# Adding the sums of squares on VectorE instead of GpSimd in a two-block transformer kernel

## The chip, the core and the metric

The program runs on one core of a Trainium2 chip. The core has engines that run side by side and wait for each other through semaphores: TensorE (PE in the rows; PEld is its weight load), VectorE (DVE), ScalarE (ACT), GpSimd (POOL) and SyncE (SP, which here only issues DMAs). The metric is the device time of one execution in microseconds, as the median of three.

## What is computed

Two transformer blocks in float32 on 256 tokens of width 1024. The first has a mixer with two attentions and a gated feed-forward with a short convolution; the second has a linear recurrence (`hgrn2_mixer`), a SwiGLU, a block attention (`moba_mixer`) and another SwiGLU. What matters here is that each section ends in a residual sum and begins with a norm over the 1024 features, so that a sum of squares over features is wanted at each border:

```python
def rms_norm(x, g):
    xf = x.astype(jnp.float32)
    y = xf * lax.rsqrt(jnp.mean(xf * xf, axis=-1, keepdims=True) + RMS_EPS)
    return (y * g.astype(jnp.float32)).astype(x.dtype)

def second_block(...):
    h = rmsnorm_of_first_block            # the first block ends in a norm of its own
    for layer in range(2):
        y = rms_norm(h, norm_mix[layer])
        y = hgrn2_mixer(y, ...) if layer == 0 else moba_mixer(y, ...)
        h = h + y
        h = h + swiglu(rms_norm(h, norm_ffn[layer]), w13[layer], w2[layer])
    return rms_norm(h, final_norm)
```

Inside `hgrn2_mixer` the output of the recurrence is normed in the same way (`rms_norm(o, out_norm)`).

## The kernel before

The residual `h` stays in SBUF turned over: features on the partitions, tokens along the free axis, as 8 slices of 128 x 256. Matrix products are made of three passes with a high and a low half of each operand (`mm3`, or `proj_w` with the halves of the input side by side). A weight block of 128 x 1024 is fetched by a DMA of SP into a buffer `f`, ScalarE writes its high half and VectorE its low half (`r<-f` on ACT, then `r<-f,r` on DVE, both 128 x 1024). `Weights` asks for these blocks some way ahead.

Six sections follow each other: `mixer1`, `ffn` with the convolution, `mixer2` (the recurrence), `ffn`, `mixer3`, and a last `ffn`, which ends in `finish` and is not touched. The other five end in `end`. It adds four pieces of the result to `h` (DVE, `h<-ps,h`, after a factor in `mixer2`), writes the high half of the next section's input, times the gain, on ACT and its low half on DVE (`r<-h,vec,r`; 128 x 256, eight of them), and calls `squares`: ACT squares `h` in four pieces of 128 x 512, three adds bring them to one, `over_partitions` adds its two halves (128 x 256) and lets TensorE sum over the partitions by 16 small passes with a column of ones (`ps<-ones,f`), `mean_rsqrt` makes the factor of each token with some ten tiny VectorE steps (`fs`, 128 x 2), and `bcast` spreads it over the partitions by two matmuls (`ps<-f,ones`). The next section's matmuls need the halves of the input at once, and the factor only later, on their results.

Before the change these adds are GpSimd's, 3 x 128 x 512 and one 128 x 256 at each of the five ends. At the end of the first `ffn` the norm of the first block and the first norm of the second come together: `squares` is called twice there, and the second call's adds are VectorE's already. In `mixer2`, three more GpSimd adds of 128 x 512 join the squares of the four pairs of heads, and `over_partitions` is VectorE's there.

No order is written by hand: every instruction is first recorded (`Trace.add`), with the earlier ones it depends on, and then `schedule` plays all of them through a list scheduler, where each has a price (`price`) and the older one goes first when two are ready. What comes out is the order of each engine's queue, and each queue runs strictly in that order on the chip. GpSimd's adds have the price

```python
            op.cost = 1000 + 4 * n if len(reads) > 1 else 150 + 2.1 * n
```

in ns for n elements of the free axis, VectorE's `69 + 1.042 * n`. A recorded instruction may be held behind one more: while `nc.floor` is set to an instruction, all that are recorded depend on it. `store_rel`, which builds the table of attention biases for `mixer3` with DMAs of GpSimd and one product on TensorE, is held in this way behind the last GpSimd instruction of `mixer1`.

All instructions are issued in `emit`, and so the profile gives nearly all of them the line L434; they are told apart by their tiles and sizes.

Of the kernel before, what the change touches and what calls it, by code (L numbers as in the profile page):

```python
# [13 lines left out]
ALU = mybir.AluOpType  # L14
# [467 lines left out]
class Builder:  # L482
# [85 lines left out]
        nc.scalar.activation(b, ps, AF.Copy)  # L568
        return b

    def squares(self, scale=None, eng=None):

        nc = self.nc
        tot = None
        for i in range(4):
            ks = slice(2 * i, 2 * i + 2)
            sq = self.t("f2", 2, SEQ)
            if scale is None:
                nc.scalar.activation(sq, self.h[:, ks, :], AF.Square)
            else:  # L580
                for k in (0, 1):
                    nc.scalar.activation(sq[:, k, :], self.h[:, 2 * i + k, :], AF.Square, scale=scale[:, 2 * i + k:2 * i + k + 1])
            if tot is None:
                tot = sq
            else:
                (eng or nc.gpsimd).tensor_tensor(tot, tot, sq, op=ALU.add)
        return self.over_partitions(tot, eng or nc.gpsimd)

    def over_partitions(self, tot, eng):

        ss, v = self.ps(2), self.t("f1", SEQ)
        eng.tensor_tensor(v, tot[:, 0], tot[:, 1], op=ALU.add)
        for t in range(2):
            for q in range(0, P, 32):
                self.nc.tensor.matmul(ss[q:q + 32, t:t + 1], lhsT=v[:, t * P + q:t * P + q + 32], rhs=self.ones[:, :1],
                                      start=True, stop=True)
        return ss
# [36 lines left out]
    def end(self, accs, g, scale=None, norm=None):  # L634


        nc = self.nc
        X, _ = self.parts(KD)
        if norm is not None:
            both = self.t("fs", KD)  # L640
            nc.vector.tensor_tensor(both, g, norm, op=ALU.mult)
            g = both
        for i in range(4):
            ks = slice(2 * i, 2 * i + 2)
            hv = self.h[:, ks, :]
            add = accs[i]
            if scale is not None:
                add = self.t("f2", 2, SEQ)
                nc.vector.tensor_tensor(add, accs[i], scale[:, None, :].to_broadcast([P, 2, SEQ]), op=ALU.mult)
            nc.vector.tensor_tensor(hv, add, hv, op=ALU.add)  # L650
            for k in (2 * i, 2 * i + 1):
                nc.scalar.activation(X[k][:, 0], self.h[:, k, :], AF.Copy, scale=g[:, k:k + 1])
                nc.vector.scalar_tensor_tensor(X[k][:, 1], self.h[:, k, :], g[:, k:k + 1], X[k][:, 0].bitcast(F32),
                                               op0=ALU.mult, op1=ALU.subtract)
        r = self.mean_rsqrt(self.squares())
        if norm is not None:

            ss, v = self.squares(norm, nc.vector), self.t("fs", 2)
            nc.vector.tensor_tensor(v, r, r, op=ALU.mult)
            nc.vector.scalar_tensor_tensor(v, ss, RS / D, v, op0=ALU.mult, op1=ALU.mult)  # L660
            nc.vector.tensor_scalar(v, v, RS * EPS, None, op0=ALU.add)
            r2 = self.rsqrt(v, 2)
            r1 = self.bcast(r)
            nc.vector.tensor_tensor(r2, r2, r, op=ALU.mult)
            out = X, r2, self.bcast(r2)
            for k in range(KD):
                nc.vector.scalar_tensor_tensor(self.h[:, k, :], self.h[:, k, :], norm[:, k:k + 1], r1, op0=ALU.mult, op1=ALU.mult)
            return out
        return X, r, self.bcast(r)
# [425 lines left out]


    def ffn(self, X, w_up, w_down, conv=False, final=False, **end):

        nc = self.nc
# [56 lines left out]
        if not final:  # L1156
            down(NB - 2, NB - 1)
            return self.end(accs, **end)
# [43 lines left out]
    def mixer2(self, X):  # L1202


        nc, a = self.nc, self.a
        V, A_, T, G = nc.vector, nc.scalar, nc.tensor, nc.gpsimd
# [5 lines left out]
        sq = self.t("f2", 2, SEQ)  # L1212
# [24 lines left out]
        def sides(p):  # L1237
            W = Weights(self, self.rows(w_in, 2 * D + p * 256, 2 * D + p * 256 + 256))
            ps = self.ps(2, 256)
            self.proj_x(W, [ps[:, 0], ps[:, 1]], X, KD, 256, one_bank=True)  # L1240
            it = self.t("f2", 2, 256)
            for t in range(2):
                A_.activation(it[:, t, :], ps[:, t, :], AF.Identity, scale=rs[:, t:t + 1])
            og = proj(3 * D + p * 256)
            A_.activation(og, og, AF.Sigmoid)
            return it, og
# [59 lines left out]
        def outs(p, sc, it, og):  # L1306
            po = self.ps(2, SEQ)
            for e in range(2):
                hc = slice(e * P, (e + 1) * P)
                T.matmul(po[:, e, :], lhsT=it[:, 0, hc], rhs=sc[:, e, :SEQ], start=True, stop=False, skip_group_check=True)  # L1310
                T.matmul(po[:, e, P:], lhsT=it[:, 1, hc], rhs=sc[:, e, SEQ:], start=False, stop=True, skip_group_check=True)
            fin = self.t("f2", 2, SEQ)
            for e in range(2):
                hd = 2 * p + e
                V.scalar_tensor_tensor(fin[:, e, :], po[:, e, :], gon[:, hd:hd + 1], og[:, e, :], op0=ALU.mult, op1=ALU.mult)
            gx, g = self.pair()
            self.hl(g[:, :, 0], g[:, :, 1], fin)
            GO.append(gx)
            if p == 0:
                A_.activation(sq, po, AF.Square)  # L1320
            else:
                o2 = self.t("f2", 2, SEQ)
                A_.activation(o2, po, AF.Square)
                G.tensor_tensor(sq, sq, o2, op=ALU.add)

        for p in range(4):
            sc = scores(p, *front(p))
            outs(p, sc, *sides(p))
        ro = self.bcast(self.mean_rsqrt(self.over_partitions(sq, V)))
        accs = self.new_accs()  # L1330
        for u in range(4):
            self.out_t(accs, w_out, u, GO[u], u == 0, u == 3)
# [78 lines left out]
def build(tc, a, out, stop=None):  # L1411
    with ExitStack() as ctx:
        b = Builder(tc.nc, a, out)

        def stopped(name):
            if stop == name:
                ht = b.tokens()
                for t in range(2):
                    b.nc.sync.dma_start(out[t * P:(t + 1) * P, :], ht[t])
                b.nc.emit(tc, ctx)  # L1420
            return stop == name

        X = b.setup()
        X = b.mixer1(X)
        end = b.nc.last("gpsimd")
        b.late_setup()
        b.nc.floor = end
        b.store_rel()
        b.nc.floor = None
        if stopped("h1"):  # L1430
            return
        if stop == "h2":
            b.ffn(X, a["w_up"][0], a["w_down"][0], conv=True, g=b.vec("norm_mix_2", 0))
            stopped("h2")
            return
        X = b.ffn(X, a["w_up"][0], a["w_down"][0], conv=True, g=b.vec("norm_mix_2", 0), norm=b.vec("norm_final_g"))
        if stopped("x2"):
            return
        X = b.mixer2(X)
        if stopped("h3"):  # L1440
            return
        X = b.ffn(X, a["ffn_w13_2"][0], a["ffn_w2_2"][0], g=b.vec("norm_mix_2", 1))
        if stopped("h4"):
            return
        X = b.mixer3(X)
        if stopped("h5"):
            return
        b.ffn(X, a["ffn_w13_2"][1], a["ffn_w2_2"][1], final=True)
        b.nc.emit(tc, ctx)
# [25 lines left out]
```

## Time and profile before

| | us |
|---|---|
| median of 3 runs (lowest, highest) | 1027.95 (1027.83, 1028.59) |
| the profiled execution | 1028.07 |
| its span, from the first to the last instruction | 1026.3 |
| PE busy in it | 999.1 (97%) |
| DVE, ACT, POOL busy | 774.5, 577.7, 42.6 |

The profile tells for each engine when each instruction began and ended, and what ended the idle time before it. TensorE's matmuls overlap in its pipeline, so that a matmul lasts longer in the rows than the distance to the next one. The views used below are the page's first part, the table of waits, tables of busy time by stretches of the span, groups of equal instructions, and the timeline, in which equal neighbours are one row. The five section ends lie at about 191, 382, 529, 719 and 825 us.

### The profile page before, as it was taken

What the parts mean: (1) busy time and instruction counts of PE and PEld (TensorE: products, weight loads), DVE (VectorE), ACT (ScalarE), POOL (GpSimd) and SP (SyncE); (2) the same over time, 40 slices, a digit from 0 to 9 for tenths busy, and PEclk for the clock granted to TensorE, in tenths of its full rate; (3) what the DMA queues carried; (4) which work ended last, traced back from release to release, by engine and by line L of the source; (5) the groups of instructions that cost most, each with busy time, mean ns of one, the idle gap of its engine ahead of it and who ended that gap; (6) DMA issues with size and microseconds to landing.
All of it is one profiled execution on the core that took longest, in us unless ns stands there. A gap on an engine that the chain in (4) does not pass through costs nothing.

```text
span 1026.3 us, 18746 instructions
## 1 busy us (share of the span) xinstructions
PE 999.1 (97%) x7526; PEld 907.1 (88%) x7526; DVE 774.5 (75%) x1434; ACT 577.7 (56%) x960; POOL 42.6 (4%) x41
## 2 busy tenths in 40 slices
PE   7999999999999999999999999999999999999996
PEld 5887899889999998999998999999889988888885
DVE  6998578699888889876878776767846586576774
ACT  7886646556656576444565445455554655545432
POOL 1000000210000002000011000000200020000000
PEclk9999999999999999999999999999999999999999
DMA  9245367377465663644554765657354745556501
GB/s 333 80 145 184 103 190 225 124 242 242 153 207 187 201 199 90 184 146 138 160 178 144 244 192 180 199 171 226 104 161 149 232 148 153 183 176 196 164 1 42
DMA packets 130152, 173.90 MB, mean 169 GB/s; under 512 B 5842, under 2 KB 112730, under 8 KB 129936
## 3 DMA queue, kind: packets, MB, share of 16 engines
q1 hardware_dynamic: 129312, 169.31, 52.5%
q0 software_dynamic: 752, 3.38, 1.0%
q8 instruction: 59, 0.97, 0.4%
q14 instruction: 29, 0.24, 0.1%
HBM read 171.61 MB, written 2.63 MB: 170 GB/s over the span
## 4 chain that ended last, share of the span: by engine, by line
PE 89%; DVE 9%; issue 1%; ACT 1%; DMA 1%; POOL 0%; DVEq 0%; POOLq 0%; ACTq 0%
PE ps L434 89%; DVE r L434 4%; DVE f L434 3%; DVE fs L434 1%; DVE h L434 1%; DMA f<-in_conv_w_dram 1%; ACT f L434 1%; POOL f L434 0%; ACT r L434 0%; DVEq L434 0%; DVE lb L434 0%; POOLq L434 0%; ACTq L434 0%; POOLq L1462 0%
## 5 line engine op out<-in xcount | busy, mean ns | idle before, releaser
L434 PE MATMUL ps<-r,r 128*128 128x256 f32 (+2 forms) x5998 | 926.4, 314 | 8.1 <-DVE r L434 7.5
L434 PEld LDWEIGHTS ps<-r,r 128*128 128x128 f32 x5998 | 834.3, 190 | 81.9 <-DVE r L434 11.1
L434 DVE TENSOR_TENSOR r<-f,r 128x1024 fp32r<-128x1024 f32 (+3 forms) x369 | 414.3, 1150 | 69.6 <-ACT r L434 33.9
L434 ACT ACTIVATE r<-f 128x1024 fp32r<-128x1024 f32 (+3 forms) x373 | 351.1, 980 | 118.9 <-PE ps L434 54.9
L434 ACT ACTIVATE f<-ps 128x256 f32<-128x256 f32 (+5 forms) x226 | 85.5, 424 | 190.5 <-PE ps L434 190.2
L434 DVE TENSOR_TENSOR f<-ps,f 128x256 f32<-128x256 f32 (+1 forms) x178 | 76.0, 460 | 80.5 <-ACT f L434 64.5
L434 DVE TENSOR_TENSOR f<-f,f 128x512 f32<-128x512 f32 (+3 forms) x153 | 100.6, 658 | 12.1 <-ACT f L434 5.5
L434 ACT ACTIVATE f<-f 128x512 f32<-128x512 f32 (+5 forms) x82 | 45.1, 551 | 49.4 <-DVE f L434 48.9
L434 POOL TENSOR_TENSOR f<-f,f 128x512 f32<-128x512 f32 x18 | 26.9, 1494 | 768.5 <-ACT f L434 459.1
L434 DVE SCALAR_TENSOR_TENSOR f<-f,cw,f 128x255 f32<-128x255 f32 (+1 forms) x88 | 38.3, 480 | 10.8 <-ACT f L434 10.7
L434 PE MATMUL ps<-f,f 128*64 128x128 f32 (+4 forms) x320 | 46.3, 330 | 0.1
L434 PEld LDWEIGHTS ps<-f,f 128*64 128x64 f32 (+3 forms) x320 | 35.7, 168 | 6.7 <-issue 2.1
L434 PE MATMUL ps<-pack,f 128*128 128x128 f32 (+2 forms) x165 | 27.5, 293 | 6.5 <-DMA f<-in_conv_w_dram 3.6
L434 ACT ACTIVATE f<-f,fs 128x256 f32<-128x256 f32 (+3 forms) x50 | 24.3, 489 | 16.7 <-DVE fs L434 16.5
L434 ACT ACTIVATE f<-f,vec,cw 128x256 f32<-128x256 f32 x44 | 23.9, 594 | 16.7 <-DVE f L434 16.7
L434 PEld LDWEIGHTS ps<-pack,f 128*128 128x128 f32 (+2 forms) x165 | 20.2, 147 | 11.1 <-DVE f L434 4.8
L434 DVE CUSTOM_DVE_ANT_0 f<-ps,f 128x256 f32<-128x256 f32 (+1 forms) x48 | 17.8, 399 | 14.2 <-PE ps L434 14.1
L434 ACT ACTIVATE f<-ps,fs 128x512 f32<-128x512 f32 (+3 forms) x28 | 15.9, 597 | 19.9 <-PE ps L434 18.8
L434 DVE SCALAR_TENSOR_TENSOR r<-h,vec,r 128x256 fp32r<-128x256 f32 x32 | 23.3, 763 | 2.0 <-ACT r L434 2.0
L434 ACT ACTIVATE r<-h,vec 128x256 fp32r<-128x256 f32 x32 | 14.5, 500 | 15.9 <-DVE h L434 15.9
L434 DVE TENSOR_TENSOR f<-f,fs 128x512 f32<-128x512 f32 (+6 forms) x46 | 16.6, 389 | 7.2 <-PE ps L434 6.7
L434 PEld LDWEIGHTS ps<-f 128*32 128x32 f32 (+2 forms) x880 | 14.0, 114 | 4.3
(85 smaller groups left out, 244.2 us busy)
## 6 DMA issues: line engine op xcount, KB each, us to landing
f<-in_ffn_w_dram SPq DMA_DIRECT2D x132, 512.0 KB, 4.2
f<-in_w_up_dram SPq DMA_DIRECT2D x44, 512.0 KB, 4.7
f<-in_hgrn_w_in_dram SPq DMA_DIRECT2D x32, 512.0 KB, 4.3
f<-in_w_in_dram SPq DMA_DIRECT2D x26, 512.0 KB, 4.9
f<-in_moba_w_in_dram SPq DMA_DIRECT2D x24, 512.0 KB, 4.5
f<-in_w_down_dram SPq DMA_DIRECT2D x22, 512.0 KB, 4.2
f<-in_w_out_dram SPq DMA_DIRECT2D x8, 512.0 KB, 3.9
f<-in_hgrn_w_out_dram SPq DMA_DIRECT2D x8, 512.0 KB, 3.3
```

The costliest lines, as they stand in the source:

```text
L434: getattr(getattr(self.nc, op.eng), op.fn)(*args, **kwargs)
```

## The change

The adds of `squares`, of `over_partitions` and of the recurrence are issued on VectorE. `squares` notes the last VectorE instruction recorded when it is called and holds its three adds behind that one: in the first call that is the low half of the eighth input slice, in the second call (at the first `ffn`'s end) the last step of the first call's factor. `store_rel` is held behind the last TensorE instruction of `mixer1`, which is the second matmul of `bcast`, instead of the last GpSimd one.

```diff
-    def squares(self, scale=None, eng=None):
+    def squares(self, scale=None):
         nc = self.nc
-        tot = None
+        tot, before = None, nc.last("vector")
...
             if tot is None:
                 tot = sq
             else:
-                (eng or nc.gpsimd).tensor_tensor(tot, tot, sq, op=ALU.add)
-        return self.over_partitions(tot, eng or nc.gpsimd)
-
-    def over_partitions(self, tot, eng):
+                nc.floor = before
+                nc.vector.tensor_tensor(tot, tot, sq, op=ALU.add)
+                nc.floor = None
+        return self.over_partitions(tot)
+
+    def over_partitions(self, tot):
         ss, v = self.ps(2), self.t("f1", SEQ)
-        eng.tensor_tensor(v, tot[:, 0], tot[:, 1], op=ALU.add)
+        self.nc.vector.tensor_tensor(v, tot[:, 0], tot[:, 1], op=ALU.add)
...
-            ss, v = self.squares(norm, nc.vector), self.t("fs", 2)
+            ss, v = self.squares(norm), self.t("fs", 2)
...
-                G.tensor_tensor(sq, sq, o2, op=ALU.add)
+                V.tensor_tensor(sq, sq, o2, op=ALU.add)
...
-        ro = self.bcast(self.mean_rsqrt(self.over_partitions(sq, V)))
+        ro = self.bcast(self.mean_rsqrt(self.over_partitions(sq)))
...
-        end = b.nc.last("gpsimd")
+        end = b.nc.last("tensor")
         b.late_setup()
         b.nc.floor = end
         b.store_rel()
```

The scheduler makes a new order of it. VectorE's queue at the end of `mixer1`, before; `r_83` holds the last two of the eight input slices, `r_92` and `r_81` are low halves of weight blocks, `f_107` is the next section's first result:

```order
L434 TENSOR_TENSOR h_170<-ps_154,h_170 128x512
L434 TENSOR_TENSOR r_87<-f_69,r_95 128x1024
L434 SCALAR_TENSOR_TENSOR r_83<-h_170,vec_182,r_83 128x256 x2
L434 TENSOR_TENSOR r_92<-f_65,r_79 128x1024
L434 TENSOR_TENSOR r_81<-f_64,r_80 128x1024
L434 TENSOR_TENSOR f_107<-ps_157,f_116 128x256
L434 TENSOR_TENSOR f_107<-ps_159,f_121 128x256
L434 TENSOR_SCALAR fs_136<-ps_153 128x2
```

The same place after the change, with the adds into `f_110` and the halves added into `f_121`:

```order
L434 TENSOR_TENSOR h_170<-ps_154,h_170 128x512
L434 TENSOR_TENSOR r_87<-f_69,r_95 128x1024
L434 SCALAR_TENSOR_TENSOR r_83<-h_170,vec_182,r_83 128x256 x2
L434 TENSOR_TENSOR f_110<-f_110,f_103 128x512
L434 TENSOR_TENSOR f_110<-f_110,f_105 128x512
L434 TENSOR_TENSOR r_92<-f_65,r_79 128x1024
L434 TENSOR_TENSOR f_110<-f_110,f_109 128x512
L434 TENSOR_TENSOR f_107<-ps_157,f_125 128x256
L434 TENSOR_TENSOR f_121<-f_110 128x256
L434 TENSOR_TENSOR f_107<-ps_159,f_116 128x256
L434 TENSOR_TENSOR r_82<-f_64,r_80 128x1024
L434 TENSOR_SCALAR fs_136<-ps_153 128x2
```

What stood up to the last input slice stands as it did; the four adds came in behind it, two of them ahead of the first weight half.

VectorE's queue at the end of the first `ffn`, before; `r_94` and `r_97` hold input slices five to eight, `f_103` is the second call's sum:

```order
L434 SCALAR_TENSOR_TENSOR r_94<-h_170,fs_132,r_94 128x256 x2
L434 TENSOR_TENSOR r_89<-f_66,r_82 128x1024
L434 SCALAR_TENSOR_TENSOR r_97<-h_170,fs_132,r_97 128x256 x2
L434 TENSOR_TENSOR r_87<-f_58,r_98 128x1024
L434 TENSOR_TENSOR f_103<-f_103,f_104 128x512
L434 TENSOR_TENSOR r_90<-f_68,r_76 128x1024
L434 TENSOR_TENSOR f_103<-f_103,f_107 128x512
L434 TENSOR_SCALAR fs_138<-ps_159 128x2
L434 TENSOR_TENSOR f_103<-f_103,f_102 128x512
```

After the change, where `r_91` and `r_90` hold these slices and `f_111` is the first call's sum:

```order
L434 SCALAR_TENSOR_TENSOR r_91<-h_170,fs_132,r_91 128x256 x2
L434 TENSOR_TENSOR r_82<-f_65,r_92 128x1024
L434 SCALAR_TENSOR_TENSOR r_90<-h_170,fs_132,r_90 128x256 x2
L434 TENSOR_TENSOR r_97<-f_64,r_81 128x1024
L434 TENSOR_TENSOR f_111<-f_111,f_105 128x512
L434 TENSOR_TENSOR r_84<-f_66,r_98 128x1024
L434 TENSOR_TENSOR f_111<-f_111,f_109 128x512
L434 TENSOR_TENSOR f_111<-f_111,f_110 128x512
L434 TENSOR_TENSOR f_123<-f_111 128x256
L434 TENSOR_TENSOR r_76<-f_68,r_89 128x1024
L434 TENSOR_SCALAR fs_138<-ps_157 128x2
```

The first call's adds took the place of the second call's, which moved behind the tiny steps of the first factor.

TensorE's queue at the end of the second block's first `ffn`, before, around the small passes with the ones:

```order
L434 MATMUL ps_155<-r_87,r_80 128x256 x2
L434 MATMUL ps_155<-r_87,r_96 128x256
L434 MATMUL ps_155<-r_87,r_80 128x256
L434 MATMUL ps_154<-ones_178,f_123 32x1 x8
L434 MATMUL ps_155<-r_87,r_80 128x256
```

After the change:

```order
L434 MATMUL ps_154<-r_80,r_82 128x256
L434 MATMUL ps_156<-r_81,r_79 128x256 x2
L434 MATMUL ps_156<-r_81,r_84 128x256
L434 MATMUL ps_156<-r_81,r_79 128x256 x2
L434 MATMUL ps_156<-r_81,r_84 128x256
L434 MATMUL ps_155<-ones_178,f_123 32x1 x8
```

They stand six matmuls behind the start of a new accumulation now, and stood ten behind it before.

## Rows read from the trace of the kernel before

**Rows 1.** The page's first part: busy us, share of the span, instructions.

```profile
PE 999.1 (97%) x7526; PEld 907.1 (88%) x7526; DVE 774.5 (75%) x1434; ACT 577.7 (56%) x960; POOL 42.6 (4%) x41
```

**Rows 2.** Five section ends: stretch, length, busy PE, PEld, DVE, ACT, POOL; clock, DMA.

```profile
190.85:212.30 21.45, 19.97 (x136) 16.69 (x136) 18.83 (x35) 11.95 (x22) 7.22 (x7) 1.00 0.32 104
382.31:405.60 23.29, 20.85 (x199) 20.28 (x198) 22.24 (x55) 14.77 (x27) 5.64 (x4) 1.00 0.34 100
528.86:551.00 22.14, 20.39 (x139) 17.07 (x138) 20.47 (x37) 12.62 (x22) 5.26 (x4) 1.00 0.45 139
718.61:737.00 18.39, 17.07 (x153) 16.54 (x152) 13.71 (x29) 10.12 (x18) 6.01 (x4) 1.00 0.35 103
825.43:844.00 18.57, 17.08 (x122) 14.69 (x121) 17.55 (x31) 10.66 (x20) 5.87 (x4) 1.00 0.44 131
sum 103.84, PE 95.36 PEld 85.27 DVE 92.79 ACT 60.12 POOL 30.01; mean PE 19.07 PEld 17.05 DVE 18.56 ACT 12.02 POOL 6.00
```

**Rows 3.** The same view, sum over the five stretches between those ends.

```profile
sum 704.40, PE 704.40 PEld 645.75 DVE 515.10 ACT 374.81 POOL 5.53; mean PE 140.88 PEld 129.15 DVE 103.02 ACT 74.96 POOL 1.11
```

**Rows 4.** Table of waits: who waited for whom, us in total, times, longest.

```profile
PE ps L434 <- DVE r L434: 7.5, 8, 1.8
```

**Rows 5.** Timeline, end of `mixer1`: start, us, engine, operation, count, [idle before, releaser].

```profile
195.31 3.75 DVE L434 SCALAR_TENSOR_TENSOR r<-h,vec,r 128x256 fp32r<-128x256 f32 x4
...
195.79 2.98 POOL L434 TENSOR_TENSOR f<-f,f 128x512 f32<-128x512 f32 x2 [179.55 <-DVE r L434]
...
201.24 3.76 PE L434 MATMUL ps<-r,r 128*128 128x512 f32 x19 [1.40 <-DVE r L434]
...
201.50 3.99 DVE L434 TENSOR_TENSOR r<-f,r 128x1024 fp32r<-128x1024 f32 x2
```

**Rows 6.** DVE groups by form: count, busy us, mean ns, idle before.

```profile
L434 DVE TENSOR_TENSOR f<-f,f 128x512 f32<-128x512 f32 x137 | 95.1, 694 | 12.0 <-ACT f L434 5.5 <-PE ps L434 4.6
...
L434 DVE SCALAR_TENSOR_TENSOR r<-h,vec,r 128x256 fp32r<-128x256 f32 x32 | 23.3, 763 | 2.0 <-ACT r L434 2.0
...
L434 DVE SCALAR_TENSOR_TENSOR h<-h,vec,f 128x256 f32<-128x256 f32 x8 | 3.7, 477 | 0.0
```

**Rows 7.** Timeline, end of the first `ffn`.

```profile
386.27 4.21 POOL L434 TENSOR_TENSOR f<-f,f 128x512 f32<-128x512 f32 x3 [162.15 <-ACT f L434]
386.36 0.68 DVE L434 TENSOR_TENSOR h<-ps,h 128x512 f32<-128x512 f32 x1
...
391.49 1.34 DVE L434 SCALAR_TENSOR_TENSOR r<-h,fs,r 128x256 fp32r<-128x256 f32 x2
...
392.49 2.41 PE L434 MATMUL ps<-r,r 128*128 128x256 f32 x18 [1.82 <-DVE r L434]
392.75 1.21 DVE L434 TENSOR_TENSOR r<-f,r 128x1024 fp32r<-128x1024 f32 x1
...
397.61 0.30 PE L434 MATMUL ps<-ones,f 128*32 128x1 f32 x16 [0.62 <-DVE f L434]
```

**Rows 8.** Timeline, end of the second `ffn`.

```profile
731.60 0.31 PE L434 MATMUL ps<-ones,f 128*32 128x1 f32 x16 [0.71 <-POOL f L434]
```

**Rows 9.** Timeline of PE alone, a stretch of equal matmuls.

```profile
385.95 4.60 PE L434 MATMUL ps<-r,r 128*128 128x256 f32 x37
```

**Rows 10.** PE groups by form: count, busy us, mean ns, idle before.

```profile
L434 PE MATMUL ps<-r,r 128*128 128x256 f32 x4340 | 567.1, 284 | 2.4 <-DVE r L434 2.4
L434 PE MATMUL ps<-r,r 128*128 128x512 f32 x1586 | 396.7, 393 | 4.5 <-DVE r L434 4.5
```

**Rows 11.** Busy time of DVE alone, nine tiny steps; stretch, length, busy.

```profile
207.28:209.04 1.76, 1.45 (x11) 1.00 0.82 256
```

**Rows 12.** DMA issues by line: count, KB each, median us to landing.

```profile
f<-in_c_rel_dram POOLq DMA_DIRECT2D x1, 96.0 KB, 4.3
```

**Rows 13.** Timeline of PE alone in `mixer2`, two levels of the recurrence.

```profile
417.88 0.45 PE L434 MATMUL ps<-f 128*32 128x16 f32 x32
...
419.52 0.45 PE L434 MATMUL ps<-f 128*32 128x16 f32 x32
```

## The prediction

> **What bounds the kernel now.** I read the page's first part, then busy time by stretches, then the waits and the timeline. PE is busy for 97% of the span, DVE for 75%, POOL for 4% [rows 1]: the time is PE's, and a change of additions can move it only where PE stands still. The five section ends last 103.84 us and hold 95.36 of PE's work, so 8.48 us of idle time; the stretches between them are 704.40 us long and PE is busy for all of it [rows 2, 3]. Two things follow. What is saved at an end goes straight to the end of the program, for nothing else is late behind it. And a new wait is not absorbed either. PE's granted clock is 1.00 at all five ends, the 2.4 GHz level, so that the stops have not cost clock and none is to be won back.
>
> Nearly all of the 8.48 is nine stops. PE waits 7.5 us for DVE's `r` in eight stops, seven of them here [rows 4]: 1.40 at the end of `mixer1` and 1.82 at the first `ffn`'s are the ones shown [rows 5, 7]. What they wait for is the low half of an input slice. Then there are .62 for the first call's half add, VectorE's work being late [rows 7], and .71 for GpSimd's half add [rows 8]. 7.5 + .62 + .71 is 8.83; one of the eight, about .5, is elsewhere, and 8.3 remain.
>
> Why is the input late? The four `r<-h,vec,r` at the end of `mixer1` took 3.75 us from 195.31 on, while two adds of POOL ran from 195.79 for 2.98 [rows 5]. Their mean over the kernel is 763 ns, while the same operation of the same size with three inputs into `h` takes 477 [rows 6]. Two weight halves, `r<-f,r`, took 3.99 there, and one without POOL beside it 1.21 [rows 5, 7]. Each of these has two inputs in SBUF. `h<-ps,h`, with one input in PSUM, took .68 in the middle of POOL's adds [rows 7]. So DVE's instructions with two SBUF inputs wait for POOL's add to end, and the chain to the input slices, which PE has nothing to do without, is stretched by them.
>
> The Trainium skill says the same in "SBUF — State Buffer", section "Who interferes with whom": VectorE with two SBUF inputs and GpSimd reading SBUF take turns on a lock that is held for a whole instruction, and one input from PSUM is outside it. The trace agrees (3.75 us for four, .68 for the PSUM form).
>
> **What is taken away.** All additions of POOL at the five ends (30.01 us of POOL there [rows 2]), and with them what they hold up. At `mixer1`'s end the four slices cost 4 x .48 = 1.9 instead of 3.75, 1.85 us earlier, and PE waited 1.40 for the last of them. At the first `ffn`'s end two slices took 1.34 right before the 1.82 stop, with others blocked ahead of them. A shown stop is not all that a stop costs. Matmuls of 128x256 follow at (4.60 - .28)/36 = .12 us [rows 9], and one lasts .28 [rows 10], so that .16 of the last one before a stop is counted as busy; and the 18 behind the 1.82 stop took 2.41 [rows 7], where 17 x .12 + .28 is 2.32, .09 for the refill. .25 for each of nine is 2.3. **Gross: 8.3 + 2.3 = 10.6 us**, if all nine go; 8.3 if my reading of the overlap is wrong.
>
> **What is added.** DVE gets at each end three adds of 128x512 at .69 [rows 6] and a half add, which none of these rows shows: it has half the elements, between .35 and .69; I take .43, since a fixed part stays. That is 2.5 an end, 12.5 in all, and 2.1 in `mixer2`. Against it stand 32 x (763 - 477) ns = 9.2 us that the slices get back [rows 6], and the blocked weight halves, 3.99 - 2 x 1.21 = 1.6 at one end [rows 5, 7]. So DVE carries about what it carried: the 92.79 us busy at the ends [rows 2], 89%, were in part waiting. In the new order the adds stand behind the last input slice, at `mixer1` with one weight half among them; the slices themselves have nothing new ahead of them. I cost the adds at nothing except where something waits for their result or for what is queued behind them. I walked the new order with these durations against PE's; what I find late:
>
> - `mixer1`'s end: the sum is there as PE reaches its small passes (0 to .5), the factor's spreading waits about as it did. I take 0.
> - `store_rel`: its DMA now waits behind the second matmul of `bcast` instead of the last GpSimd add, which itself stood ahead of that. Landing takes 4.3 us [rows 12]. PE's product on the table comes about 4.5 us of its work later, with only some .2 to spare. It costs 0 to 1; I take .25.
> - First `ffn`'s end: the first call's adds now stand where the second call's were, the second's behind the tiny steps. Between the second sum and its factor DVE has eight products for `h` (8 x .48 = 3.8), four weight halves (4 x 1.21 = 4.8) and some ten tiny steps (2.0, from nine in 1.76 [rows 11]): 10.6. PE's order has 73 matmuls of 128x256 and the small passes in that stretch, 73 x .12 + .3 = 9.1. That makes 1.5 at most; 0 if DVE does some of the products while the squares are still coming. I take .7, near the middle, since the instructions overlap a little on DVE too.
> - `mixer2`'s end: up to one weight half (1.21) stands between the tiny steps; 0 to 1.2, I take .5. The last two ends show none.
> - `mixer2` itself: three adds go to DVE, 2.1 us over a stretch of 120 us, and a level of the recurrence needs a product of DVE: I take .3, 0 to 2.
>
> The new waits sum to .25 + .7 + .5 + .3 = 1.75, between 0 and 5.2. **Net: 10.6 - 1.75 = 8.85 us.** 1028.07 - 8.85 = 1019.2 for the profiled execution; the median lies .12 lower, which is nothing here. The gain ends at 10.6 or, with the upper bounds of all waits and 8.3, at 3.1: 1017.5 to 1025.
>
> **The rivals.** *A: VectorE becomes the last to arrive.* It is busy for 89% of the ends already, and a 2.5 us block is put ahead of weight halves there. If at each end one weight half (1.21) then comes late at PE, five times, 6.0 of 10.6 go: 4.6, with the small waits 3: 1023.5 to 1025. Against it: the between stretches have DVE busy for 515.10 of 704.40 us and no PE idle, so the weights are ahead of PE [rows 3]; for it: the wait of .7 above is of this kind.
>
> The Trainium skill's "Perfetto Trace Analysis", section "Optimizing Scalar/DVE Operations", would lighten a saturated VectorE by giving work to ScalarE or even GpSimd, which is the other way round from this change; the same section doubts it between VectorE and GpSimd, for they share a port. Rows 5 to 7 bear out the doubt.
>
> *B: slower, by the recurrence.* The new order starts the recurrence of the first two pairs of heads some 8 us of PE work later, so that its levels meet the weight halves of the following products. A level follows another on PE in 419.52 - 417.88 = 1.64 us [rows 13]. If in each of 16 levels a weight half (1.21) stands ahead of the level's product (.69, as an add of that size) on DVE, and PE's next pass (.45) follows only then, a level lasts 2.35 and PE loses .7: 11.4 in all. With 1.75 of other waits the sum is +2.5: 1030.6. It decides from .55 a level on, 8.85/16. Against it: PE's 1.64 a level against .45 of its own passes leaves 1.2 of other products as fill, and no stop is seen there before [rows 3].
>
> *C: nothing changes.* Were the long slices not POOL's doing, or were something next to them late by as much (ACT's high halves, the arrival of weights), the stops would stay: 1026.5 to 1029. Against it is the contrast of .68 for the PSUM form and .94 a piece (3.75 for four) beside the same adds.
>
> **How the numbers follow.** The forecast, nine stops gone and about 1.75 us of new waits, .80. A .11, B .05, C .04. The range of 8 in 10 runs from 1016.5, a little below the full gain since small waits of `bcast` could go too, to 1024, inside A and short of the 1025 of all upper bounds together; beyond it lie much of A, B and C and a sliver of the forecast. A measurement of this kernel tells .2%, 2 us, from no change: faster .91 (forecast and A), same .04 (C), slower .05 (B).
>
> **What would show it.** Right: `r<-h,vec,r` at a mean near 480 ns instead of 763; DVE's `r` no longer among PE's large waits; PE idle at the ends about 2 instead of 8.48; POOL's row with almost nothing; DVE's adds of 128x512 at 155 (18 more), still .69 each. Wrong: slices at 480 and PE waiting for DVE's `r<-f,r` or `fs` instead (A); PE's passes `ps<-f` of the levels more than 2 us apart (B); slices still near 760 (C). A product on the table late by more than 1 us would put the loss into `store_rel`.

## The result, and the profile after

The changed kernel takes 1016.77 us (1016.58 to 1016.92, four runs) against 1028.15 (1027.83 to 1028.59) of the kernel before: the ratio is 0.9888, with a 95% interval of 0.9875 to 0.9901. The forecast was 1019.2, between 1016.5 and 1024; the direction and the range held, and the gain of 11.4 us is 2.5 larger than the 8.85 forecast, and the time lies only .27 us above the lower end of the range.

The page's first part, and under it the sum of the five section ends in the table by stretches (length, then busy time), to be set beside [rows 1, 2]:

```profile
PE 996.2 (98%) x7526; PEld 907.5 (89%) x7526; DVE 769.5 (76%) x1457; ACT 576.5 (57%) x960; POOL 9.4 (1%) x18
```

```profile
190.85:209.80 18.95, 18.95 (x137) 17.13 (x136) 17.10 (x36) 11.14 (x21) 1.05 (x2) 1.00 0.39 130
...
sum 92.55, PE 92.55 PEld 86.40 DVE 83.20 ACT 61.45 POOL 1.05; mean PE 18.51 PEld 17.28 DVE 16.64 ACT 12.29 POOL 0.21
```

The stretches are the ones of before, cut at the same matmuls (by their number in PE's queue). The ends lasted 103.84 us and last 92.55: 11.29 us less, which is the gain. PE is busy for all of that time; the 8.48 us of idle time are gone without a rest. VectorE has 23 instructions more and is busy for less: 83.20 us at the ends instead of 92.79, 769.5 in all instead of 774.5. The groups of VectorE by form tell why, against [rows 6]:

```profile
L434 DVE TENSOR_TENSOR f<-f,f 128x512 f32<-128x512 f32 x155 | 106.5, 689 | 11.8 <-ACT f L434 5.2 <-PE ps L434 4.4
...
L434 DVE SCALAR_TENSOR_TENSOR r<-h,vec,r 128x256 fp32r<-128x256 f32 x32 | 14.3, 481 | 2.1 <-ACT r L434 2.1
...
L434 DVE TENSOR_TENSOR f<-f 128x256 f32<-128x256 f32 x11 | 4.6, 422 | 0.1
```

The half adds of the kernel before:

```profile
L434 DVE TENSOR_TENSOR f<-f 128x256 f32<-128x256 f32 x6 | 2.5, 422 | 1.2 <-POOL f L434 1.2
```

18 more adds of 128x512 at .69, five more half adds at .42, and the input slices at 481 ns instead of 763. The timeline at the end of `mixer1` shows the four slices that took 3.75 us [rows 5] in 1.71, and the two adds behind the last slice:

```profile
195.36 1.71 DVE L434 SCALAR_TENSOR_TENSOR r<-h,vec,r 128x256 fp32r<-128x256 f32 x4
...
198.72 0.88 DVE L434 SCALAR_TENSOR_TENSOR r<-h,vec,r 128x256 fp32r<-128x256 f32 x2
199.52 1.41 DVE L434 TENSOR_TENSOR f<-f,f 128x512 f32<-128x512 f32 x2
200.85 1.22 DVE L434 TENSOR_TENSOR r<-f,r 128x1024 fp32r<-128x1024 f32 x1
```

In the table of waits, where `DVE r` stood with 7.5 us in eight stops and `POOL f` with .7 [rows 4, 8], this is all that is left for PE (who waited for whom, us in total, times, longest):

```profile
PE ps L434 <- DMA f<-in_conv_w_dram: 3.6, 1, 3.6
PE ps L434 <- DMA pack<-in_c_pack_dram: 3.0, 1, 3.0
PE ps L434 <- DVE f L434: 2.8, 3, 1.6
PE ps L434 <- ACT r L434: 0.9, 2, 0.5
PE ps L434 <- DVE r L434: 0.5, 1, 0.5
```

None of these lies at a section end. The one of .5 is the eighth stop of before, which stands in `mixer1`.

### The profile page after: what moved, and what is told of

It is laid out like the page before. It is cut to its first block, busy times and chain, and to the rows that moved or that the text cites. A ratio compares the mean times of both kernels' runs of the same rounds, so it can differ in the third digit from the quotient of the medians.

```text
span 1014.6 us, 18707 instructions
## 1 busy us (share of the span) xinstructions
PE 996.2 (98%) x7526; PEld 907.5 (89%) x7526; DVE 769.5 (76%) x1457; ACT 576.5 (57%) x960; POOL 9.4 (1%) x18
## 4 chain that ended last, share of the span: by engine, by line
PE 95%; DVE 3%; DMA 1%; ACT 0%; issue 0%; DVEq 0%; ACTq 0%; POOLq 0%
PE ps L434 95%; DVE f L434 2%; DVE fs L434 1%; DMA f<-in_conv_w_dram 1%; ACT f L434 0%; DVE r L434 0%; DVE lb L434 0%; DVEq L434 0%; ACTq L434 0%; POOLq L1465 0%
## 5 line engine op out<-in xcount | busy, mean ns | idle before, releaser
L434 DVE TENSOR_TENSOR r<-f,r 128x1024 fp32r<-128x1024 f32 (+3 forms) x369 | 409.4, 1136 | 77.0 <-ACT r L434 37.5
L434 DVE TENSOR_TENSOR f<-f,f 128x512 f32<-128x512 f32 (+3 forms) x171 | 112.2, 658 | 11.9 <-ACT f L434 5.2
L434 PE MATMUL ps<-f 128*32 128x16 f32 (+3 forms) x880 | 17.7, 191 | 0.0
L434 DVE SCALAR_TENSOR_TENSOR r<-h,vec,r 128x256 fp32r<-128x256 f32 x32 | 14.3, 481 | 2.1 <-ACT r L434 2.1
```

Of the source, the lines that this page charges most:

```text
L434: getattr(getattr(self.nc, op.eng), op.fn)(*args, **kwargs)
```

## The experiments

The theory is the prediction's: while GpSimd adds two tiles, VectorE's instructions with two SBUF inputs stand still, and the slices that PE waits for come late. The rivals: that the sum of squares simply came too late from a slow engine; that the scheduler's new order did it; and, for what it means elsewhere, that any work of GpSimd disturbs, or that VectorE has no room for the adds.

**GpSimd's adds put back, with nobody waiting for them.**

```diff
                 nc.vector.tensor_tensor(tot, tot, sq, op=ALU.add)
                 nc.floor = None
+                if scale is None:
+                    nc.gpsimd.tensor_tensor(self.t("dm", 2, SEQ), sq, sq, op=ALU.add)
```

The scheduler prices this addition at 1 ns, as every instruction of these runs that writes the tile `dm`, so that it moves nothing else.

> The changed kernel with 15 additions of 128x512 put back on GpSimd, three at each of the five section ends, on the same squares as VectorE's adds, into a tile that nobody reads; nobody waits for them, and the order of the instructions on TensorE, VectorE and ScalarE is the changed kernel's. Theory (GpSimd's add holds up VectorE's two-input instructions): r<-h,vec,r goes back from 481 ns to 700 or more, the stops of TensorE come back, 1022 to 1030 us, likeliest 1026. Rival (the gain came from the sum being ready earlier or from the new order, not from what ran beside it): 1016.8 +- 1.

Measured: 1027.52 us against 1028.57 of the kernel before on the same chip, a ratio of 0.9986 (0.9977 to 0.9996). Of the gain a tenth is left, though no result of GpSimd is used and the three other engines run the same instructions in the same order. The timeline at the end of `mixer1` shows the mechanism in three rows (start, length; in brackets PE's idle time and what ended it):

```profile
195.43 3.23 DVE L436 SCALAR_TENSOR_TENSOR r<-h,vec,r 128x256 fp32r<-128x256 f32 x4
...
195.91 2.47 POOL L436 TENSOR_TENSOR dm<-f 128x512 f32<-128x512 f32 x2 [179.55 <-DVE r L436]
...
200.85 4.21 PE L436 MATMUL ps<-r,r 128*128 128x512 f32 x22 [0.90 <-DVE r L436]
...
205.82 0.30 PE L436 MATMUL ps<-ones,f 128*32 128x1 f32 x16 [0.76 <-DVE f L436]
```

The slices take 3.23 us instead of 1.71 and end .28 after GpSimd's second add (198.66 against 198.38). PE stops for the input (.90) and again for the sum (.76), since VectorE has its own adds behind the delay. Over the kernel the slices' mean is 660 ns, short of the 700 expected, and the two lines of the table of waits stand against .5 and 2.8 us in the changed kernel:

```profile
PE ps L436 <- DVE f L436: 7.0, 8, 1.6
...
PE ps L436 <- DVE r L436: 3.7, 7, 0.9
```

So the larger part of this run's stops is for the sum, 4.2 us more against 3.2 for the input, where the kernel before waited mostly for the input, 7.0 us at the ends against 1.3 for sums [rows 4, 7, 8]. What is shown is that GpSimd's adds hold up VectorE's two-input work, whichever of it PE waits for. The rival by the new order falls, and so does the one by the slow sum as the only cause: the sum is VectorE's here.

**The same with one input.** 
```diff
+                if scale is None:
+                    nc.gpsimd.tensor_scalar(self.t("dm", 2, SEQ), sq, 2.0, None, op0=ALU.mult)
```

> The same with a GpSimd instruction of one SBUF input, tensor_scalar 128x512, about as long as the add (1.57 us for one of this size at the end of the kernel). Theory, if it is GpSimd reading SBUF that counts: much the same loss as with the adds, 1021 to 1030. Rival (only a GpSimd instruction with two inputs holds VectorE up): 1016.8 +- 1.

Measured: 1019.42, a ratio of 0.9911 (0.9896 to 0.9925). It missed both: neither the loss of the adds nor nothing, but some 2.4 us. At the end of `mixer1`:

```profile
195.12 2.02 DVE L436 SCALAR_TENSOR_TENSOR r<-h,vec,r 128x256 fp32r<-128x256 f32 x4
195.61 3.31 POOL L436 TENSOR_SCALAR dm<-f 128x512 f32<-128x512 f32 x2 [179.55 <-DVE r L436]
...
197.66 1.46 DVE L436 TENSOR_TENSOR r<-f,r 128x1024 fp32r<-128x1024 f32 x1
199.04 1.26 DVE L436 SCALAR_TENSOR_TENSOR r<-h,vec,r 128x256 fp32r<-128x256 f32 x2
```

GpSimd works for 3.31 us beside VectorE, and VectorE goes on: four slices 2.02 instead of 1.71, a weight half 1.46 instead of 1.22, two slices 1.26 instead of .88. Each meeting costs VectorE about .3, not the length of the other's instruction.

The Trainium skill, "SBUF — State Buffer", "Who interferes with whom", has a VectorE instruction with two SBUF inputs contend with a GpSimd instruction that reads SBUF, over ports that it calls an exclusive lock. With two operands on GpSimd's side the trace agrees (3.23 us for four slices, which end .28 behind GpSimd's second add); with one, the delays are .3 and not the 1.7 us of GpSimd's instruction, and here the measurement decides.

**The same with memsets, which read nothing.** Three of 128x512 for each add. In a first try nothing on GpSimd made them wait for the section end:

```diff
+                if scale is None:
+                    dm = self.t("dm", 2, SEQ)
+                    nc.floor = nc.last("scalar")
+                    for _ in range(3):
+                        nc.gpsimd.memset(dm, 0.0)
+                    nc.floor = None
```

> The same with three GpSimd memsets of 128x512 (540 ns each) in the place of each add, which read nothing. Theory (the reads matter): 1016.8 +- 1, r<-h,vec,r stays near 481 ns. Rival (writing counts as well, or any work of GpSimd): 1021 to 1030.

Measured: 1018.02 (0.9896, 0.9881 to 0.9911). The memsets ran in two blocks away from the slices, so that the run tells nothing of the ends. The next expectation has all of them at the start of the kernel; that holds for the first block alone. The 1.2 us above the changed kernel lie ahead of the first end; what they come from is not shown.

```profile
16.29 5.22 POOL L436 MEMSET dm<- 128x512 f32 x9
...
232.82 21.00 POOL L436 MEMSET dm<- 128x512 f32 x36
```

The second try puts a small instruction ahead that reads the squares:

```diff
+                if scale is None:
+                    dm = self.t("dm", 2, SEQ)
+                    nc.gpsimd.tensor_scalar(dm[:, 0, :2], sq[:, 0, :2], 2.0, None, op0=ALU.mult)
+                    nc.floor = nc.last("gpsimd")
+                    for _ in range(3):
+                        nc.gpsimd.memset(dm, 0.0)
+                    nc.floor = None
```

> The fills again, now made to run at the section ends: ahead of each three memsets GpSimd scales two columns of the squares that the add reads, and so has to wait for them. In the first try (idle_pool_fill) nothing made the fills wait and they ran at the start of the kernel. The order on TensorE, VectorE and ScalarE is the changed kernel's. Theory (GpSimd's reads matter): at most .5 over the changed kernel, 1016.3 to 1017.5, r<-h,vec,r at 480 to 500 ns. Rival (writing counts as well): 1019 or more, r<-h,vec,r over 550.

Measured: 1016.56 (0.9884, 0.9869 to 0.9899), the changed kernel's time. GpSimd is busy for 42.3 us, as much as in the kernel before (42.6), and the fills run beside the slices:

```profile
195.26 1.71 DVE L436 SCALAR_TENSOR_TENSOR r<-h,vec,r 128x256 fp32r<-128x256 f32 x4
195.75 0.46 POOL L436 TENSOR_SCALAR dm<-f 128x2 f32<-128x2 f32 x1 [179.57 <-DVE r L436]
196.27 1.69 POOL L436 MEMSET dm<- 128x512 f32 x3
```

1.71 us, nothing lost. A GpSimd that is busy with writing alone is harmless here; one that reads is not.

**VectorE's room.** Each add at the ends is followed by one of the same size into a tile that nobody reads:

```diff
                 nc.vector.tensor_tensor(tot, tot, sq, op=ALU.add)
                 nc.floor = None
+                if scale is None:
+                    nc.floor = before
+                    nc.vector.tensor_tensor(self.t("dm", 2, SEQ), sq, sq, op=ALU.add)
+                    nc.floor = None
```

> The changed kernel with VectorE's three adds of each of the five section ends doubled: the second of each pair goes into a tile that nobody reads and is held behind the last input slice like the first. 15 x .69 = 10.3 us more on VectorE. If VectorE has cover left behind the slices, as the empty idle time of TensorE says: 1016.8 to 1020, likeliest 1018.5. If VectorE is the next to be late (rival A of the prediction): 1021 to 1027.

Measured: 1022.44 (0.9940, 0.9925 to 0.9955). This went to rival A: 5.7 us of the 10.3 show. All five small passes stop now, these two the longest and the shortest:

```profile
541.75 0.30 PE L436 MATMUL ps<-ones,f 128*32 128x1 f32 x16 [1.30 <-DVE f L436]
...
726.65 0.31 PE L436 MATMUL ps<-ones,f 128*32 128x1 f32 x16 [0.96 <-DVE f L436]
```

How little room the changed kernel has can be read from its own rows, too. At the end of `mixer1` the half add is through at 203.34 and the passes start at 203.75:

```profile
202.92 0.42 DVE L434 TENSOR_TENSOR f<-f 128x256 f32<-128x256 f32 x1
...
203.75 0.31 PE L434 MATMUL ps<-ones,f 128*32 128x1 f32 x16
```

At the five ends these distances are .30 to .43 us. The adds fit, but with little to spare.

**The parts of the change.** In `ends_only` the recurrence's three adds stay on GpSimd, in `mix2_only` they alone go to VectorE; the first diff is to the changed kernel, the second to the kernel before.

```diff
-                V.tensor_tensor(sq, sq, o2, op=ALU.add)
+                G.tensor_tensor(sq, sq, o2, op=ALU.add)
```

```diff
-                G.tensor_tensor(sq, sq, o2, op=ALU.add)
+                V.tensor_tensor(sq, sq, o2, op=ALU.add)
```

> The changed kernel with the recurrence's three adds left on GpSimd. Theory (the gain lies at the section ends, mixer2 had .1 us of idle time on TensorE before): 1016.8 +- 1. Rival (the recurrence's adds carried part of the gain): 1018.5 or more.

> The kernel before with only the recurrence's three adds on VectorE. Theory: 1028.1 +- 1. Rival: 1026.5 or less; or, by the prediction's rival B, 1029.5 or more if the recurrence on VectorE gets late.

Measured: 1016.54 (0.9878, 0.9864 to 0.9893) and 1028.95 (1.0002, 0.9992 to 1.0011). The recurrence's adds carry nothing; the whole gain is the section ends'. `no_hold` leaves out the hold of the adds; in `rel_early`, `store_rel` is held behind the half add, noted in `over_partitions`:

```diff
-                nc.floor = before
                 nc.vector.tensor_tensor(tot, tot, sq, op=ALU.add)
-                nc.floor = None
```

```diff
         self.nc.vector.tensor_tensor(v, tot[:, 0], tot[:, 1], op=ALU.add)
+        self.half = self.nc.last("vector")
...
-        end = b.nc.last("tensor")
+        end = b.half
```

> The changed kernel without holding the adds behind the last VectorE instruction: the scheduler may put them between the input slices. If the hold matters: one or two adds, .69 each, stand ahead of the last slices at each end, .5 to 1.4 us an end, 1019 to 1024. If the slack at the slices (the stops of 1.4 to 1.8 us went with 1.9 us or more) is enough, or the scheduler puts them behind anyway: 1016.8 +- 1.

> The changed kernel with store_rel held behind the half add of mixer1's end, as it was before by GpSimd's half add, instead of behind the second matmul of bcast. The prediction gave .25 us, 0 to 1, to this: 1015.8 to 1016.8 if the hold costs that; 1016.8 +- .5 if it costs nothing, which the gapless TensorE after mixer1 says.

Measured: 1016.80 (0.9881, 0.9865 to 0.9898) and 1017.01 (0.9884, 0.9869 to 0.9899), both the changed kernel's time. Without the hold the scheduler did put one add ahead of the last two slices at the end of `mixer1`, and PE did not stop for it:

```profile
198.34 0.68 DVE L434 TENSOR_TENSOR f<-f,f 128x512 f32<-128x512 f32 x1
...
200.08 0.87 DVE L434 SCALAR_TENSOR_TENSOR r<-h,vec,r 128x256 fp32r<-128x256 f32 x2
```

**Only the half adds on GpSimd**, in the five calls of `over_partitions` that were GpSimd's.

```diff
-        self.nc.vector.tensor_tensor(v, tot[:, 0], tot[:, 1], op=ALU.add)
+        (eng or self.nc.gpsimd).tensor_tensor(v, tot[:, 0], tot[:, 1], op=ALU.add)
```

> The changed kernel with only the half add (128x256) of the five section ends on GpSimd: 1.26 us instead of .42, and up to 1.2 us of VectorE's two-input work held up behind the slices. 1017 to 1020, likeliest 1018: the .71 us stop for it at the second ffn's end comes back, others have a few tenths of cover. If every sum is on the path: 5 x (.84 + .25) = 5.5 us, 1022.

Measured: 1016.74 (0.9885, 0.9871 to 0.9900): nothing lost, below what was expected. The scheduler knows GpSimd's price and puts the small passes later, 205.84 at the end of `mixer1` instead of 203.75; the half add, behind all the slices, has 2 us more. So the half add's slowness alone costs nothing where the passes are placed for it.

**GpSimd's adds, but late.** In `pool_late` the adds and half adds of the five ends are GpSimd's again, recorded with the hold of the changed kernel.

```diff
                 nc.floor = before
-                nc.vector.tensor_tensor(tot, tot, sq, op=ALU.add)
+                (nc.gpsimd if scale is None else nc.vector).tensor_tensor(tot, tot, sq, op=ALU.add)
                 nc.floor = None
```

> The changed kernel with the adds of the five section ends on GpSimd as before, but held behind the last input slice, so that they can't hold up the slices. Three adds of 1.5 and a half add of 1.3 make 5.8 us instead of 2.5, and weight halves beside them are still held up. Theory (the stops came from slices that were held up): most of the gain stays, 1017 to 1021. Rival (GpSimd's adds are simply too slow for the sum, or the held-up weight halves count as much): 1023 or more.

Measured: 1026.36 (0.9983, 0.9973 to 0.9992). By the expectation's numbers this is the rival's, but the kernel did not do what it was made for. The adds were not late:

```profile
195.29 3.74 DVE L434 SCALAR_TENSOR_TENSOR r<-h,vec,r 128x256 fp32r<-128x256 f32 x4
195.77 2.98 POOL L434 TENSOR_TENSOR f<-f,f 128x512 f32<-128x512 f32 x2 [179.56 <-DVE r L434]
...
200.69 0.87 DVE L434 SCALAR_TENSOR_TENSOR r<-h,vec,r 128x256 fp32r<-128x256 f32 x2
...
201.22 6.77 PE L434 MATMUL ps<-r,r 128*128 128x512 f32 x36 [1.39 <-DVE r L434]
```

The last two slices begin at 200.69, five us behind the add that is held behind them. The hold shapes the order in which the scheduler writes the queues down; it puts no wait on the chip, and on an engine of its own nothing else keeps the order. All seven stops for `DVE r` are there again as in the kernel before; only the small passes, which the scheduler moved back, stop no more. `pool_gated` makes the wait real: GpSimd first scales two columns of the last slice's low half.

```diff
+        if gate is not None:
+            nc.gpsimd.tensor_scalar(self.t("dm", 2, SEQ)[:, 0, :2], gate[:, :2], 2.0, None, op0=ALU.mult)
+            before = nc.last("gpsimd")
...
-        r = self.mean_rsqrt(self.squares())
+        r = self.mean_rsqrt(self.squares(gate=X[KD - 1][:, 1].bitcast(F32)))
```

> The adds of the five section ends on GpSimd as before, and now really behind the last input slice: GpSimd first scales two columns of that slice's low half, and so waits for it; in pool_late the hold was one of the scheduler's alone, and the adds ran as in the kernel before. Theory (the slices held up were what stopped TensorE): r<-h,vec,r at 480 to 500 ns, TensorE's stops for DVE r gone, 1017 to 1021; what is left of the loss is weight halves held up and late sums. Rival (GpSimd's adds are too slow for the sum, or hold up the weight halves by as much): 1023 or more.

Measured: 1024.70 (0.9958, 0.9944 to 0.9972). Each theory got half. The slices are back at 480 ns and no stop for `DVE r` is left at the ends, as the theory says; but the time is the rival's, for the sums are late. PE waits 6.6 us for them, 2.0 of it at the end of `mixer1`:

```profile
199.15 2.35 DVE L436 TENSOR_TENSOR r<-f,r 128x1024 fp32r<-128x1024 f32 x2
199.33 2.26 POOL L436 TENSOR_SCALAR dm<-r 128x2 f32<-128x2 f32 x1 [183.39 <-DVE r L436]
201.57 5.73 POOL L436 TENSOR_TENSOR f<-f,f 128x512 f32<-128x512 f32 x3
...
208.16 0.31 PE L436 MATMUL ps<-ones,f 128*32 128x1 f32 x16 [2.03 <-POOL f L436]
```

The turn-taking goes both ways: GpSimd's two columns took 2.26 us, until VectorE's two weight halves were through. Some 2 us of the lateness at four of the five ends are therefore the gate's own, and at these four PE's stops for the sum (2.03, 1.30, .42 and 1.16) are hardly longer than that. What the run does show is that the stops for the input go when GpSimd keeps off the slices; whether GpSimd's adds without a gate would then be too slow for the sum it does not show.

## Why the prediction was right, and where its sizes were off

- *What bounded the kernel* (idle time at the ends passes straight to the end of the program): right. The ends became 11.29 us shorter, and the time fell by 11.38. [Rows 3] is not the whole between the ends: it leaves out 512.7 to 528.86 us and takes in the last 2.9 us of the first end. Over the whole, with the last stretch up to 1016 us, PE is busy for all but .09, so that the reading stands:

```profile
sum 721.31, PE 721.22 PEld 662.60 DVE 525.48 ACT 383.35 POOL 6.82; mean PE 144.24 PEld 132.52 DVE 105.09 ACT 76.67 POOL 1.36
```

- *The cause* (two SBUF inputs against GpSimd's adds): shown by the adds that nobody waits for, with memsets as the control. It is the section ends alone, by `ends_only` and `mix2_only`.
- *The gross gain* of 8.3 + 2.3: all nine stops went, and two waits of .09 and .10 ahead of `bcast`s with them, which the forecast had left standing: 8.48 in all. PE's busy time at the ends fell from 95.36 to 92.55, by 2.81 and not 2.3. A wait of .09 hides as much as a long one. Before the change, at the end of `mixer1`, PE was through at 209.29:

```profile
205.17 4.12 PE L434 MATMUL ps<-r,r 128*128 128x512 f32 x24
209.38 0.71 PE L434 MATMUL ps<-f,ones 128*128 128x128 f32 x4
```

After it, without the wait, the four matmuls of `bcast` take .61 (211.09 in the rows for `store_rel`). That is .10 for the refill; with the .16 of the matmul ahead it comes to .26, where the forecast had .25. So the size of a stop was good, and what was short is the count. Nine such stops, seven for the input and two at the `bcast`s, make 2.3; the rest of the 2.81, with the two stops ahead of the small passes, was not told apart. Together 11.29 instead of 10.6.
- *The adds at nothing* on VectorE: right. Its busy time fell by 5 us, where the forecast had it about unchanged.
- *The new waits* of 1.75: this is the term that failed, each of its four parts was 0. The largest was .7 for the second factor at the first `ffn`'s end. Its two counts were good: VectorE needed 10.4 us from the second half add to the factor's last step (10.6 forecast), PE 9.1 to the `bcast`. But they do not start together:

```profile
397.81 0.43 DVE L434 TENSOR_TENSOR f<-f 128x256 f32<-128x256 f32 x1
...
399.20 0.31 PE L434 MATMUL ps<-ones,f 128*32 128x1 f32 x16
...
407.70 0.48 DVE L434 TENSOR_SCALAR f<-pack,fs 128x128 f32<-128x128 f32 x2
...
408.29 0.61 PE L434 MATMUL ps<-f,ones 128*128 128x128 f32 x4
```

The sum was ready at 398.24, one us before PE came to its small passes, and the factor at 408.18, .1 before PE needed it. The forecast had walked the new order with VectorE and PE level at that point. At `mixer2`'s end, as at all five, PE is never idle, and of the recurrence's .3 nothing shows: `ends_only`, where its adds stay on GpSimd, takes the same time.
- *`store_rel`* at .25, because its DMA would wait behind the second `bcast` matmul: wrong in the mechanism too. In the changed kernel that DMA is issued at 206.66 and PE's first `bcast` matmul starts at 211.09. The hold is the scheduler's, and `rel_early` and the changed kernel take the same time.

```profile
206.66 0.55 POOL L434 DMA_DIRECT2D f<-in_c_rel_dram  x1 [190.36 <-DVE fs L434]
...
211.09 0.61 PE L434 MATMUL ps<-f,ones 128*128 128x128 f32 x4
```

- *The range*: its sum of upper bounds is wrong. The five waits' .5, 1, 1.5, 1.2 and 2 make 6.2, not 5.2, so that by its own terms the smallest gain is 2.1 us and the longest time 1026. The measured time is at the other end. The two errors of size went the same way, 1.75 us of waits that did not come and .7 of gross gain that did, and the range held since it had been drawn past the full gain for just such waits of `bcast`.
- *Rival A* is not what happened, but `idle_dve_add` shows it was near: another three adds on VectorE at each end, and half the gain is gone.
- *Rival B* falls. The levels of the recurrence follow each other as before (1.64 us [rows 13]):

```profile
418.48 0.45 PE L434 MATMUL ps<-f 128*32 128x16 f32 x32
...
420.12 0.45 PE L434 MATMUL ps<-f 128*32 128x16 f32 x32
```

- *Rival C* falls with the slices at 481 ns.

## What to carry to other kernels

Before an addition is given to an idle GpSimd, look at what VectorE does at that moment: if it is at two-input work in SBUF that another engine waits for, GpSimd's 1.5 us come on top of it, although the share of busy time says that GpSimd is free. The sign in a profile is one group of equal VectorE instructions with a mean far above that of a like group (763 against 477 ns), and rows that end a quarter of a us after GpSimd's. And when the work moves to VectorE, read how long before its use each result is ready (here .30 to .43 us at the five ends), and try by dummy work what happens when that is used up.

## What was not expected of the hardware

- A GpSimd instruction with one SBUF input did not stop VectorE's two-input instructions for its length; each meeting cost about .3 us (2.02 instead of 1.71 for four slices), and 15 such instructions cost the kernel 2.4 us, against some 10 for 15 adds.
- GpSimd waited for VectorE in turn, and not always for one instruction alone: in `pool_gated` a scaling of 128x2 took 2.25 to 2.26 us at four ends, behind two weight halves of 2.35 together, and 1.12 at the fifth, behind the first of two. In `fill_gated` fourteen of fifteen such scalings took .21 to .74, most of them to the end of the one VectorE instruction under way, and one took 2.43. What decides between the two is not shown. The short one of `pool_gated`:

```profile
538.85 1.12 POOL L436 TENSOR_SCALAR dm<-r 128x2 f32<-128x2 f32 x1 [139.72 <-DVE r L436]
```

The long one of `fill_gated`:

```profile
388.81 2.43 POOL L436 TENSOR_SCALAR dm<-f 128x2 f32<-128x2 f32 x1
```

- 45 memsets of 128x512 on GpSimd, 23.7 us at the section ends, cost nothing that can be measured (1016.56 against 1016.77).
